# The ada_w partition sums: one float32 product per 512 columns, or two products on a high and a low part

## The chip, the cores and the metric

The kernel runs on one core of a Trainium2 chip. The metric is the device time of one execution in microseconds (us); the figure given is the median of several runs. A core has five engines that work side by side: TensorE (PE in the rows, with PEld for its weight loads), VectorE (DVE), ScalarE (ACT), GpSimd (POOL) and SyncE (SP, which issues most of the DMAs). Each engine takes its own instructions in the order in which the program lists them.

## The reference, cut to what matters

The program is two transformer blocks in a row over 256 tokens of width 2048: a mixer block with three branches and a feed-forward part, and a second block with four attention mixers and 16 experts. The change touches only how `mod` is made, with which the second block is modulated:

```
c_act = jax.nn.silu(c)
for l in range(DEPTH):
    mod = c_act @ ada_w[l] + ada_b[l]
    sh1, sc1, g1, sh2, sc2, g2 = jnp.split(mod, 6, axis=-1)
    h = rmsnorm_2(x, norm1_g[l]) * (1.0 + sc1[:, None]) + sh1[:, None]
    x = x + g1[:, None] * token_mixer(h, w_in[l], ...)
    ...
```

`c` has 2048 entries and `ada_w` is 2048 x 12288, so `mod` is six vectors of 2048. They depend on nothing of the first block, and the kernel computes them in the background while the first block runs.

## The kernel before, in words

Every large matrix product goes through one stream of chunks. A chunk is up to 1024 columns of one 128-row tile of a weight. SP loads the tile into a ring buffer; `_split` (L146, L147) then makes two parts of it, with the type float32r, which TensorE takes in one go: ACT casts it to a high part `wh`, and DVE subtracts that from the weight to get the low part `wl`. TensorE multiplies three times (`wh*xh`, `wh*xl`, `wl*xh`; L181 to L183, or L171 to L173 where tokens are on the partitions of the output). `run` keeps some four to five chunks split ahead of the one that TensorE works on, and after each chunk calls `step`, which takes one piece of background work from each queue: attention heads, norms, convolutions, and a queue named "ada". What `step` calls is recorded there and then, so its instructions stand in each engine's list behind the splits that are already ahead and in front of the splits still to come.

Tiles of `ada_w` are loaded in between as side loads, 96 of 1 MB each. They go through no split and no large product. For one of six groups `g`, 16 tiles are summed on DVE with the entries of `c` as factors (L1148) into `a`, a float32 tile of 128 x 2048 that holds the partial sums of each partition. When the 16th is in, `total(g)` is put on the queue "ada", two empty steps behind. `total` sums `a` over the partitions: for each of four pieces of 512 columns TensorE multiplies a column of ones with the piece (L1160; the result is one row of 512 in PSUM), and ACT copies the row back into partition 0 of `a` (L1161). GpSimd then writes the row to DRAM (L1163). This happens six times in the program, each time between two chunks of the large products.

The tags `pts` and `prob`, which the change borrows, are small tiles of 128 x 512 that the attention heads and convolutions use, four buffers each.

Of the kernel before, what the change touches and what calls it, by code (L numbers as in the profile page):

```python
# [10 lines left out]
F32 = mybir.dt.float32  # L11
F32R = mybir.dt.float32r
# [33 lines left out]
class Kernel:  # L46
# [1054 lines left out]
    def prepare2(self):  # L1101

        nc, i = self.nc, self.i
# [39 lines left out]
        def use(g, kt, wt):  # L1143
            if g == 0 and kt == 0:
                self.flush("norm", "c")
                start(0)
            a = A[g]
            nc.vector.scalar_tensor_tensor(a, wt, self.col["c"][:, kt:kt + 1], a, op0=OP.mult, op1=OP.add)  # L1148
            if kt == 15:
                if g < 5:  # L1150
                    start(g + 1)
                for f in 2 * [lambda: None] + [lambda: total(g)]:
                    self.bg("ada", f)

        def total(g):
            a = A.pop(g)
            for k in range(4):
                ps = self.bank()
                s = slice(k * 512, k * 512 + 512)
                nc.tensor.matmul(ps[0:1, :], self.ones[:, 0:1], a[:, s], start=True, stop=True)  # L1160
                nc.scalar.copy(a[0:1, s], ps[0:1, :])  # L1161
                self.done(ps)
            nc.gpsimd.dma_start(self.mod[order[g]:order[g] + 1, :], a[0:1, :])  # L1163
            self.free(a)
            if g == 1:
                self.later("ada", 2, lambda: self.setup_cols(first, 4))
            if g == 5:
                self.setup_cols(second)
# [1182 lines left out]
```

## Time and profile before

| what | value |
|---|---|
| median of 3 runs | 2854.59 us (2854.22 to 2856.4) |
| the profiled execution's own time | 2856.04 us |
| span of its instructions | 2854.3 us |
| PE busy | 2756.7 us, 97% of the span |
| DVE busy | 2106.4 us, 74% |
| ACT busy | 1418.5 us, 50% |
| POOL busy | 315.8 us, 11% |
| mean granted TensorE clock | 0.987 |

The profile is of one execution whose own time is 1.45 us above the median; 1.7 us of its time lie around the span. Busy shares are averages over stages with different limits. A matmul is recorded with a length that overlaps the next one, so the distance from the start of one to the start of the next tells what it costs in a stream. A float32 product is recorded as two matmuls, which is why L1160 has 48 records for 24 products.

### The profile page before, as it was taken

The page shows a single profiled execution, that of the slowest core. Times are in us where ns is not written, and L with a number is a line of the kernel's source. Part 1 is how long each engine was busy: PE and PEld are TensorE (multiplying, and loading weights), DVE is VectorE, ACT ScalarE, POOL GpSimd, SP SyncE. Part 2 cuts the span into 40 slices and gives each one's busy share as a digit, 9 for nine tenths or more (in the row PEclk, how much of TensorE's full clock was granted, in tenths as well). Part 3 has the DMA queues.
Part 4 walks back from the last instruction along what each step waited for, and adds up shares of the span by engine and source line. Part 5 has one row for each costly group of instructions (what it writes and reads, how often), then busy time and mean ns, then how long its engine had stood idle before and what let it go on. Part 6 is the DMA issues. An engine that isn't in the chain of part 4 may idle for free. (4 is left out here: it accounts for less than half of the span.)

```text
span 2854.3 us, 43859 instructions
## 1 busy us (share of the span) xinstructions
PE 2756.7 (97%) x17766; PEld 2410.4 (84%) x17766; DVE 2106.4 (74%) x2679; ACT 1418.5 (50%) x2100; POOL 315.8 (11%) x286
## 2 busy tenths in 40 slices
PE   8999999999999999999999998999999799999997
PEld 8898999999998999897989797988886676666664
DVE  5566558899767768877777786656555689998998
ACT  5433444334444545434444445345554476666665
POOL 0000100000100000001000102111001202222223
PEclk9999999999999999999999999999999899999999
DMA  7576555566667765676667573745555599989895
GB/s 256 193 275 247 199 215 166 176 235 214 248 233 266 259 228 221 239 263 216 257 216 267 195 253 128 265 128 195 179 202 173 209 372 337 342 324 343 322 342 211
DMA packets 201427, 685.77 MB, mean 240 GB/s; under 512 B 12148, under 2 KB 15332, under 8 KB 180356
## 3 DMA queue, kind: packets, MB, share of 16 engines
q1 hardware_dynamic: 194336, 662.94, 64.3%
q0 software_dynamic: 5680, 19.53, 2.5%
q8 instruction: 141, 2.31, 0.3%
q10 hardware_dynamic: 1203, 0.45, 0.1%
q14 instruction: 67, 0.54, 0.1%
HBM read 680.66 MB, written 2.20 MB: 239 GB/s over the span
## 5 line engine op out<-in xcount | busy, mean ns | idle before, releaser
L147 DVE TENSOR_TENSOR u<-u,u 128x1024 fp32r<-128x1024 f32 (+3 forms) x1064 | 1258.1, 1216 | 393.9 <-ACT u L146 392.2
L146 ACT CAST u<-u 128x1024 fp32r<-128x1024 f32 (+3 forms) x1064 | 1015.3, 995 | 615.6 <-DMA u<-in_w_in_dram 157.3
L181 PE MATMUL ps<-u,u 128*128 128x256 f32 (+1 forms) x2184 | 626.3, 287 | 2.6 <-ACT u L146 1.7
L183 PE MATMUL ps<-u,u 128*128 128x256 f32 (+1 forms) x2184 | 621.1, 284 | 2.5 <-DVE u L147 2.5
L182 PE MATMUL ps<-u,u 128*128 128x256 f32 (+1 forms) x2184 | 621.0, 284 | 0.5
L181 PE MATMUL ps<-big,u 128*128 128x256 f32 (+1 forms) x1672 | 481.4, 288 | 1.2 <-ACT big L1285 0.7
L183 PE MATMUL ps<-big,u 128*128 128x256 f32 (+1 forms) x1672 | 476.6, 285 | 4.3 <-DVE u L147 4.3
L182 PE MATMUL ps<-big,u 128*128 128x256 f32 (+1 forms) x1672 | 476.5, 285 | 0.1
L181 PEld LDWEIGHTS ps<-u,u 128*128 128x128 f32 (+1 forms) x2184 | 420.9, 193 | 11.9 <-issue 6.4
L183 PEld LDWEIGHTS ps<-u,u 128*128 128x128 f32 (+1 forms) x2184 | 420.7, 193 | 4.4 <-DVE u L147 4.3
L182 PEld LDWEIGHTS ps<-u,u 128*128 128x128 f32 (+1 forms) x2184 | 420.9, 193 | 1.7 <-DVE u L1286 1.3
L181 PEld LDWEIGHTS ps<-big,u 128*128 128x128 f32 (+1 forms) x1672 | 322.9, 193 | 13.5 <-issue 7.0
L183 PEld LDWEIGHTS ps<-big,u 128*128 128x128 f32 (+1 forms) x1672 | 322.9, 193 | 5.8 <-DVE u L147 5.6
L182 PEld LDWEIGHTS ps<-big,u 128*128 128x128 f32 (+1 forms) x1672 | 323.0, 193 | 1.1 <-DVE big L1286 0.6
L171 PE MATMUL ps<-u,u 128*128 128x512 f32 x736 | 291.6, 396 | 5.4 <-ACT u L146 5.3
L172 PE MATMUL ps<-u,u 128*128 128x512 f32 x736 | 288.8, 392 | 7.9 <-DVE u L147 7.5
L173 PE MATMUL ps<-u,u 128*128 128x512 f32 x736 | 287.6, 391 | 0.0
L1148 DVE SCALAR_TENSOR_TENSOR u<-u,cols,u 128x2048 f32<-128x2048 f32 x96 | 226.3, 2357 | 5.6 <-DMA u<-in_ada_w_dram 5.5
L1914 PE MATMUL ps<-u,xg 128*128 128x512 f32 x416 | 187.9, 452 | 0.4 <-DVE xg L1905 0.3
L172 PEld LDWEIGHTS ps<-u,u 128*128 128x128 f32 x736 | 138.7, 188 | 39.4 <-DVE u L147 12.4
L171 PEld LDWEIGHTS ps<-u,u 128*128 128x128 f32 x736 | 138.5, 188 | 39.5 <-ACT u L146 8.7
L1915 PE MATMUL ps<-u,xg 128*128 128x512 f32 x416 | 167.7, 403 | 0.8 <-DVE u L147 0.7
(374 smaller groups left out, 3111.5 us busy)
## 6 DMA issues: line engine op xcount, KB each, us to landing
u<-in_w_in_dram SPq DMA_DIRECT2D x128, 1024.0 KB, 5.0
u<-in_ada_w_dram SPq DMA_DIRECT2D x96, 1024.0 KB, 5.4
u<-in_w_up_dram SPq DMA_DIRECT2D x88, 1024.0 KB, 5.4
u<-in_exp_w_gate_dram SPq DMA_DIRECT2D x64, 1024.0 KB, 9.5
u<-in_exp_w_up_dram SPq DMA_DIRECT2D x64, 1024.0 KB, 6.8
u<-in_exp_w_down_dram SPq DMA_DIRECT2D x64, 1024.0 KB, 8.1
u<-in_w_down_dram SPq DMA_DIRECT2D x44, 1024.0 KB, 6.7
u<-in_w_o_dram SPq DMA_DIRECT2D x16, 1024.0 KB, 6.8
```

The costliest lines, as they stand in the source:

```text
L146: self.nc.scalar.copy(wh[:, :width], wt)
L147: self.nc.vector.tensor_sub(wl[:, :width], wt, wh[:, :width].bitcast(F32))
L171: nc.tensor.matmul(o, xh[:, ts], wh[:, cs], start=first, stop=False)
L172: nc.tensor.matmul(o, xh[:, ts], wl[:, cs], start=False, stop=False)
L173: nc.tensor.matmul(o, xl[:, ts], wh[:, cs], start=False, stop=last)
L181: nc.tensor.matmul(o, wh[:, cs], xh, start=first and m % 2 == 0, stop=False, **kw)
L182: nc.tensor.matmul(o, wh[:, cs], xl, start=False, stop=False, **kw)
L183: nc.tensor.matmul(o, wl[:, cs], xh, start=False, stop=last, **kw)
L1148: nc.vector.scalar_tensor_tensor(a, wt, self.col["c"][:, kt:kt + 1], a, op0=OP.mult, op1=OP.add)
L1914: self.nc.tensor.matmul(ps, x, wh[:, s], start=start, stop=False)
L1915: self.nc.tensor.matmul(ps, x, wl[:, s], start=False, stop=stop)
```

## The change

`total` makes a float32r column `one` out of the column of ones when it is first called. For each piece of 512 columns ACT then casts the piece to a high part `h` (in a `pts` buffer), DVE subtracts it from the piece to give a low part `l` (in a `prob` buffer), and TensorE multiplies the ones with `h` and with `l`, both summed in the same PSUM row. The copy back is as before.

```diff
         def total(g):
             a = A.pop(g)
+            if g == 0:
+                self.one = self.ctile([128, 1], "one", F32R)
+                nc.scalar.copy(self.one, self.ones[:, 0:1])
             for k in range(4):
                 ps = self.bank()
                 s = slice(k * 512, k * 512 + 512)
-                nc.tensor.matmul(ps[0:1, :], self.ones[:, 0:1], a[:, s], start=True, stop=True)
+
+                h, l = (self.small([128, 512], tag, 4, F32R) for tag in ("pts", "prob"))
+                nc.scalar.copy(h, a[:, s])
+                nc.vector.tensor_sub(l, a[:, s], h.bitcast(F32))
+                nc.tensor.matmul(ps[0:1, :], self.one, h, start=True, stop=False)
+                nc.tensor.matmul(ps[0:1, :], self.one, l, start=False, stop=True)
                 nc.scalar.copy(a[0:1, s], ps[0:1, :])
                 self.done(ps)
```

In the changed file the cast is L1165, the subtraction L1166, the two products L1167 and L1168, and the copy back L1169.

On ACT, at the first of the six sums (`u157` is the tile `a`, `u416` and `u422` are halves of chunks that are split ahead), the list before reads:

```order
L146 CAST u416_3538<-u392_3368 128x1024 [waits Activation_49]
L1161 COPY u157_1483<-ps418_3567 1x512 [waits DMASW3_49,PE_49]
L1161 COPY u157_1483<-ps419_3570 1x512 [waits PE_49]
L1161 COPY u157_1483<-ps420_3573 1x512 [waits PE_49]
L1161 COPY u157_1483<-ps421_3576 1x512 [waits PE_49]
L146 CAST u422_3580<-u404_3451 128x1024 [waits DMAHW7_49,Activation_49]
```

In the changed program the same place on ACT reads:

```order
L146 CAST u416_3538<-u392_3368 128x1024 [waits Activation_49]
L1159 CAST one_3567<-ones_77 128x1
L1165 CAST pts419_3570<-u157_1483 128x512 [waits DMASW3_49]
L1169 COPY u157_1483<-ps418_3569 1x512 [waits PE_49]
L1165 CAST pts422_3578<-u157_1483 128x512
L1169 COPY u157_1483<-ps421_3577 1x512 [waits PE_49]
L1165 CAST pts425_3586<-u157_1483 128x512
L1169 COPY u157_1483<-ps424_3585 1x512 [waits PE_49]
L1165 CAST pts428_3594<-u157_1483 128x512
L1169 COPY u157_1483<-ps427_3593 1x512 [waits PE_49]
L146 CAST u430_3602<-u404_3451 128x1024 [waits DMAHW7_49]
```

Each cast of a piece now stands behind the copy back of the piece ahead of it, and that copy waits for PE. The other five sums have the same pattern, without the cast of `one`.

On PE, at the same place, the four float32 products give way to eight, in pairs, between two chunks of the large product:

```order
-L1160 MATMUL ps418_3567<-u157_1483,ones_77 1x512 [waits DMASW3_49,DVE_49]
-L1160 MATMUL ps419_3570<-u157_1483,ones_77 1x512 [waits Activation_49]
-L1160 MATMUL ps420_3573<-u157_1483,ones_77 1x512 [waits DVE_49]
-L1160 MATMUL ps421_3576<-u157_1483,ones_77 1x512 [waits Activation_49]
+L1167 MATMUL ps418_3569<-pts419_3570,one_3567 1x512 [waits DVE_49,Activation_49]
+L1168 MATMUL ps418_3569<-prob420_3571,one_3567 1x512 [waits DVE_49]
+L1167 MATMUL ps421_3577<-pts422_3578,one_3567 1x512 [waits PE_49,Activation_49]
+L1168 MATMUL ps421_3577<-prob423_3579,one_3567 1x512 [waits DVE_49]
+L1167 MATMUL ps424_3585<-pts425_3586,one_3567 1x512 [waits Activation_49]
+L1168 MATMUL ps424_3585<-prob426_3587,one_3567 1x512 [waits DVE_49]
+L1167 MATMUL ps427_3593<-pts428_3594,one_3567 1x512 [waits Activation_49]
+L1168 MATMUL ps427_3593<-prob429_3595,one_3567 1x512 [waits DVE_49]
```

The second product of each pair waits for DVE's subtraction, and the next product of the large matrix stands behind the last of the eight.

On DVE, at the same place in the changed program, the four subtractions stand between two subtractions of the split:

```order
L147 TENSOR_TENSOR u416_3538<-u392_3368,u416_3538 128x1024 [waits Activation_49]
L1166 TENSOR_TENSOR prob420_3571<-u157_1483,pts419_3570 128x512 [waits Activation_49]
L1166 TENSOR_TENSOR prob423_3579<-u157_1483,pts422_3578 128x512 [waits Activation_49]
L1166 TENSOR_TENSOR prob426_3587<-u157_1483,pts425_3586 128x512 [waits Activation_49]
L1166 TENSOR_TENSOR prob429_3595<-u157_1483,pts428_3594 128x512 [waits PE_49,Activation_49]
L147 TENSOR_TENSOR u430_3602<-u404_3451,u430_3602 128x1024 [waits DMAHW7_49,Activation_49]
```

The first of them stands behind the split's subtraction ahead of it; before, nothing of the sums stood on DVE here.

## Rows read from the trace of the kernel before

**Rows 1.** The page's first part: busy time of PE.

```profile
PE 2756.7 (97%) x17766; PEld 2410.4 (84%) x17766; DVE 2106.4 (74%) x2679; ACT 1418.5 (50%) x2100; POOL 315.8 (11%) x286
```

**Rows 2.** Timeline of PE at the six sums: start, length, engine, line, [idle before].

```profile
361.05 3.59 PE L1160 MATMUL ps<-u,ones 128*1 128x512 f32 x8
364.57 0.39 PE L181 MATMUL ps<-u,u 128*128 128x256 f32 x1
...
784.16 3.59 PE L1160 MATMUL ps<-u,ones 128*1 128x512 f32 x8
...
1064.38 3.60 PE L1160 MATMUL ps<-u,ones 128*1 128x512 f32 x8
...
1349.33 3.59 PE L1160 MATMUL ps<-u,ones 128*1 128x512 f32 x8
...
1635.26 3.59 PE L1160 MATMUL ps<-u,ones 128*1 128x512 f32 x8
...
2014.71 3.59 PE L1160 MATMUL ps<-u,ones 128*1 128x512 f32 x8
```

**Rows 3.** Timeline of PE in a stream of float32r products of 512 columns.

```profile
1326.11 0.39 PE L172 MATMUL ps<-u,u 128*128 128x512 f32 x1
1326.33 0.39 PE L173 MATMUL ps<-u,u 128*128 128x512 f32 x1
```

**Rows 4.** Timeline of ACT, then of DVE, behind the fifth sum.

```profile
1638.88 0.58 ACT L1161 COPY u<-ps 1x512 f32<-1x512 f32 x1 [0.28 <-PE ps L1160]
1639.37 0.61 ACT L146 CAST u<-u 128x512 fp32r<-128x512 f32 x1
...
1640.01 0.69 DVE L147 TENSOR_TENSOR u<-u,u 128x512 fp32r<-128x512 f32 x1 [6.25 <-ACT u L146]
```

**Rows 5.** Timeline of DVE, then of PE, where PE waits for a subtraction.

```profile
1090.71 1.22 DVE L147 TENSOR_TENSOR u<-u,u 128x1024 fp32r<-128x1024 f32 x1
...
1091.98 0.38 PE L183 MATMUL ps<-u,u 128*128 128x256 f32 x1 [0.55 <-DVE u L147]
```

**Rows 6.** Timeline of ACT and DVE: their last work ahead of each sum.

```profile
359.96 1.03 ACT L146 CAST u<-u 128x1024 fp32r<-128x1024 f32 x1
...
361.03 1.23 DVE L147 TENSOR_TENSOR u<-u,u 128x1024 fp32r<-128x1024 f32 x1 [1.99 <-ACT u L146]
...
780.35 2.36 DVE L147 TENSOR_TENSOR u<-u,u 128x1024 fp32r<-128x1024 f32 x2 [4.62 <-ACT u L146]
...
1061.16 2.35 DVE L147 TENSOR_TENSOR u<-u,u 128x1024 fp32r<-128x1024 f32 x2
...
1350.37 2.35 DVE L147 TENSOR_TENSOR u<-u,u 128x1024 fp32r<-128x1024 f32 x2
...
1632.47 1.29 DVE L147 TENSOR_TENSOR u<-u,u 128x512 fp32r<-128x512 f32 x2
...
2011.92 1.28 DVE L147 TENSOR_TENSOR u<-u,u 128x512 fp32r<-128x512 f32 x2
```

**Rows 7.** Timeline of PE where it resumes behind waits for DVE.

```profile
692.28 0.77 PE L921 MATMUL ps<-ln,ones 128*128 128x256 f32 x1 [5.21 <-DVE ln L916]
...
1329.52 0.50 PE L172 MATMUL ps<-u,u 128*128 128x512 f32 x1 [0.99 <-DVE u L147]
```

**Rows 8.** Stretches: length, busy time of PE, PEld, DVE, ACT, POOL, PE's clock, DMA.

```profile
692.30:697.00 4.70, 4.70 (x20) 4.52 (x21) 4.31 (x3) 0.74 (x2) 0.00 (x0) 0.50 0.64 222
697.01:704.00 6.99, 6.99 (x60) 6.99 (x60) 4.47 (x3) 6.74 (x11) 0.00 (x0) 1.00 0.31 83
...
1188.97:1191.93 2.96, 2.96 (x7) 2.38 (x8) 2.96 (x3) 0.35 (x1) 0.00 (x0) 0.50 0.60 126
...
1329.50:1333.00 3.50, 3.48 (x15) 2.92 (x16) 3.50 (x3) 0.37 (x1) 0.00 (x0) 1.00 0.66 159
```

**Rows 9.** PE's waits in total: us, times, longest us.

```profile
PE ps L1836 <- DVE sel L1833: 9.5, 1, 9.5
...
PE ps L921 <- DVE ln L916: 5.2, 1, 5.2
```

## The prediction

> **What bounds the kernel now.** I began with the busy times: PE is busy 2756.7 of 2854.3 us, 97% [rows 1]. Whatever lengthens PE's list in a full stretch lengthens the kernel, and what ACT or DVE do costs only where PE comes to wait for it. Next I read PE's timeline at the six places of the change. The reader is to see that a sum stands in a full stream: at the first one the first product with the ones starts at 361.05 and the next chunk at 364.57, and no row there shows idle time; the other five look the same [rows 2]. So PE spends 3.52 us from the first product of a sum to the next chunk, six times, 21.1 us in all, and it waits for nothing there. Third, I read the timelines of ACT and DVE ahead of the sums, since the change puts them into PE's way. At four of six sums both have been idle for some time when PE arrives; at the first and the fourth DVE has just begun on splits [rows 6].
>
> **What the change removes.** Four float32 products per sum, 3.52 us of PE's time, six times [rows 2].
>
> **What it adds on PE.** Eight float32r products of 512 columns. In a stream these follow each other by 0.22 to 0.23 us [rows 3]. If nothing waited, a sum would take 8 x 0.23 = 1.84 us, 1.7 less than now.
>
> **What it adds as a wait.** The parts are not there beforehand. In ACT's list the cast of piece k+1 stands behind the copy back of piece k. That copy needs both products of piece k, and the second of them needs DVE's subtraction, which needs the cast. So four pieces go round one loop through three engines, and nothing of two pieces overlaps. The loop, from the start of one copy back to that of the next:
>
> - copy back to cast on ACT: 1638.88 to 1639.37, 0.49 us [rows 4];
> - cast of 128 x 512 and hand-off to DVE: 1639.37 to 1640.01, 0.64 us [rows 4];
> - subtraction of 128 x 512: 0.69 us [rows 4];
> - hand-off from DVE to PE: a subtraction from 1090.71 for 1.22 us, PE at 1091.98, so 0.05 us [rows 5];
> - the second product until its result can be read: 0.39 us [rows 3], and 0.04 for the hand-off, like the others.
>
> That is 2.30 us. The parts of the first piece can be made ahead of PE, and at sums 2, 3, 5 and 6 they are: DVE ends its last split at 782.71, 1063.51, 1633.76 and 2013.20, a subtraction of 0.69 later the low part is there, and PE arrives at 784.16, 1064.38, 1635.26 and 2014.71 [rows 2, 6]. There PE takes 0.23 for the first product, three loops of 2.30, 0.23 for the last product and about 0.1 to start on the next chunk: 7.4 us against 3.52, so 3.9 more.
>
> At sum 1 DVE works on a split from 361.03 for 1.23 us. A second one in a row starts 1.13 behind the first (two take 2.36, one 1.23) [rows 6], so the low part is there at 361.03 + 1.13 + 0.69 + 0.05 = 362.90, 1.85 us behind PE's arrival instead of 0.23: 1.6 on top, 5.5. ACT's cast ends at 360.99 and the cast of `one` and of the first piece fit beside DVE's split. At sum 4 DVE has two splits until 1352.72, so the low part is there at about 1353.37, 4.04 behind PE's arrival at 1349.33 [rows 2, 6]: 3.8 on top, 7.7.
>
> Sum of the loops: 4 x 3.9 + 5.5 + 7.7 = 28.8 us. Bounds: DVE's part could be a fifth longer where GpSimd works beside it, or the loop could be 0.2 shorter if hand-offs overlap. With 18 loops of 2.1 to 2.55 that is 25 to 33 us.
>
> **Edits at no cost.** The cast of `one` happens once. The buffers `pts` and `prob` have four slots each, and sums of four pieces take one round of them. The splits behind a sum are held up on ACT, but against PE they stay where they were: before, ACT's next split starts 0.6 us after PE resumes (1639.37 at the fifth sum [rows 4], where PE resumes at 1635.26 + 3.52 = 1638.78 [rows 2]); in the changed order it starts 0.49 behind the last copy back, which itself starts some 0.2 behind PE's restart, about 0.7. The chunks that PE takes meanwhile had been split ahead of the sum. If that cover were gone, PE would wait another 0.7 to 2 us per sum. The write to DRAM moves with the last copy back, and its readers come several steps later.
>
> **TensorE's clock.** During a loop PE does two products of 0.23 in 2.30 us, for some 7 us. What such a broken stretch does to the clock, the trace shows at neighbours. Behind a wait of 5.21 us PE resumed at 692.28 and ran at half clock (0.50, that is 1.2 instead of 2.4 GHz) until 697: 20 products in 4.70 us, which at full clock (60 in 6.99) take 2.3, so 2.4 us lost. Elsewhere, among waits of about 1 us for a split, PE ran at 0.50 from 1188.97 to 1191.93: 7 products of 512 in 2.96 us instead of 1.6, 1.4 lost. Yet behind a wait of 0.99 us at 1329.52 the clock stayed at 1.00 [rows 3, 7, 8]. A sum of the changed kernel is idle longer than the first of these in total, and is broken for longer than any of them, so I take the fall as likely at each of the six, at the mean of both prices, 1.9 us: 11.4 us. Bounds: 0 (as at 1329.52) and 6 x 2.4 = 14.4.
>
> The Trainium skill, "TensorE: Matmul & The Clock Gate", section "HAM oscillation — how this bites in real kernels", says that a matmul loop with idle gaps between its bursts is put back to the half clock and that each next burst then starts slow. [...]
>
> **Sum.** 28.8 + 11.4 = 40.2 us. On the profiled execution's own 2856.04 that is 2896.2; its time is 1.45 above the median, and on the median of 2854.59 it is 2894.8. I predict 2895.
>
> **Rivals.**
>
> - *The loop without the clock.* The small products keep the clock at 1.00. For it: 1329.52. Against: 692.30 and 1188.97 [rows 8]. Time: 2854.6 + 28.8 = 2883.
> - *The products get cheaper and nothing waits.* Two float32r passes for a float32 product: 1.84 against 3.52 us, 1.7 less, six times: 10 us less, 2844.5. It decides if the parts of a piece are there before PE wants them, that is if ACT casts ahead of its copies back. Against: the order on ACT, with a copy back between any two casts.
> - *The delay is taken up later.* PE has waits of 5.2 and 9.5 us for DVE behind the sums [rows 9]. If DVE came to these by its own pace, they would shrink as PE gets late: up to 14.7 us back, 2880. Against: DVE's work there uses what PE has just made, and it moves along.
> - *The splits come too late as well.* ACT and DVE take up the splits behind a sum later than PE needs them; at 1091.98 PE already waits for a split soon after the third sum [rows 5]. Four subtractions more on DVE, 2.8 us, would come on top at two or three sums: 2895 + 7 = 2902.
>
> **How the numbers follow.** Loop with clock 0.68 (2886 to 2902 by its own bounds), loop without clock 0.15, late splits 0.08, taken up later 0.04, cheaper products 0.03, no measurable change by a mixture 0.02. The range of 2881 to 2904 leaves out the last two, the strongest form of the third last and the tail of the late splits. A measurement of this kernel tells about 0.2% (5.7 us) from no change. Slower holds all but the last two: 0.95; faster 0.03; same 0.02.
>
> **What would show it.** Right: at each sum PE's timeline shows the second product of a pair waiting for DVE, pairs 2.3 us apart, and 7.4 us from the first product to the next chunk (9 and 11 at the first and fourth sum); ACT alternates cast and copy; the clock reads 0.50 behind the sums. PE's total wait for L1166 would be near 6 x 6 = 36 us. Wrong: pairs 0.5 us apart, a clock of 1.00 throughout, or shrunken waits at L921 and L1836.

## The result and the profile after

The changed kernel takes 2897.25 us (median of 4 runs, 2895.84 to 2898.7); before, beside it, 2854.56 us (4 runs). That is 42.7 us more, a ratio of 1.0147 with an interval of 1.0131 to 1.0163. The kernel before, run again beside the experiments, had medians of 2856.31 and 2856.09, so a difference between the change and an experiment is uncertain by some 2 us. The profiled execution took 2898.02 us with a span of 2896.2 us.

The page's first part answers to [rows 1]. PE is busy 12 us longer in a span that is 42 us longer; most of the loss is PE standing still.

```profile
PE 2768.5 (96%) x17766; PEld 2421.3 (84%) x17766; DVE 2123.0 (73%) x2703; ACT 1432.0 (49%) x2125; POOL 316.2 (11%) x286
```

PE's timeline at the second sum answers to the second place of [rows 2]. Columns are start, length, engine, line, tiles, shape, and in brackets the idle time ahead with its releaser.

```profile
791.85 0.28 PE L183 MATMUL ps<-u,u 128*128 128x256 f32 x1
791.97 0.40 PE L1167 MATMUL ps<-pts,one 128*1 128x512 f32 x1
792.20 0.40 PE L1168 MATMUL ps<-prob,one 128*1 128x512 f32 x1
793.79 0.40 PE L1167 MATMUL ps<-pts,one 128*1 128x512 f32 x1 [1.18 <-ACT pts L1165]
794.51 0.39 PE L1168 MATMUL ps<-prob,one 128*1 128x512 f32 x1 [0.33 <-DVE prob L1166]
796.09 0.39 PE L1167 MATMUL ps<-pts,one 128*1 128x512 f32 x1 [1.18 <-ACT pts L1165]
796.82 0.40 PE L1168 MATMUL ps<-prob,one 128*1 128x512 f32 x1 [0.34 <-DVE prob L1166]
798.39 0.58 PE L1167 MATMUL ps<-pts,one 128*1 128x512 f32 x1 [1.18 <-ACT pts L1165]
799.12 0.58 PE L1168 MATMUL ps<-prob,one 128*1 128x512 f32 x1
799.50 0.41 PE L181 MATMUL ps<-u,u 128*128 128x256 f32 x1
```

The second products of the four pairs start at 792.20, 794.51, 796.82 and 799.12, that is 2.30 to 2.31 apart. From the first product (791.97) to the next chunk (799.50) are 7.53 us, against 3.52 in [rows 2]. The first pair waits for nothing. The last two products are longer (0.58), and so are the chunk's (0.41): the clock has fallen while PE was still in the loop.

ACT at the same place, and below "..." DVE, show what goes round:

```profile
792.64 0.57 ACT L1169 COPY u<-ps 1x512 f32<-1x512 f32 x1 [2.95 <-PE ps L1168]
793.12 0.61 ACT L1165 CAST pts<-u 128x512 fp32r<-128x512 f32 x1
794.94 0.57 ACT L1169 COPY u<-ps 1x512 f32<-1x512 f32 x1 [1.21 <-PE ps L1168]
...
793.77 0.69 DVE L1166 TENSOR_TENSOR prob<-u,pts 128x512 fp32r<-128x512 f32 x1 [2.55 <-ACT pts L1165]
```

Copy at 792.64, cast 0.48 later, subtraction 0.65 after that, product at 794.51 (0.74), next copy at 794.94 (0.43): 2.30 in all. ACT sits idle for 1.21 us of each lap, with the next cast ready to go behind a copy that waits for PE.

At the fourth sum PE comes to a cast that is not there. PE's timeline, and below "..." that of ACT:

```profile
1368.08 0.28 PE L183 MATMUL ps<-big,u 128*128 128x256 f32 x1
1371.13 0.59 PE L1167 MATMUL ps<-pts,one 128*1 128x512 f32 x1 [2.77 <-ACT pts L1165]
1372.66 0.59 PE L1168 MATMUL ps<-prob,one 128*1 128x512 f32 x1 [0.94 <-DVE prob L1166]
1374.43 0.59 PE L1167 MATMUL ps<-pts,one 128*1 128x512 f32 x1 [1.18 <-ACT pts L1165]
1375.16 0.59 PE L1168 MATMUL ps<-prob,one 128*1 128x512 f32 x1
...
1380.53 0.41 PE L181 MATMUL ps<-big,u 128*128 128x256 f32 x1
...
1368.56 1.99 ACT L146 CAST u<-u 128x1024 fp32r<-128x1024 f32 x2 [6.61 <-DVE u L1071]
1370.46 0.61 ACT L1165 CAST pts<-u 128x512 fp32r<-128x512 f32 x1
```

Two split casts, 1.99 us together, stand ahead of the cast of the piece. They stood there before as well, over PE's arrival at 1349.33 [rows 2]; the timeline of ACT in the kernel before:

```profile
1348.16 1.99 ACT L146 CAST u<-u 128x1024 fp32r<-128x1024 f32 x2 [4.43 <-DVE u L1148]
```

The clock falls during PE's wait (0.59 from 1371.13 on), and the laps are longer by it: 1372.66 to 1375.16 is 2.50.

For a table of all six sums I take the time from the start of the last chunk product ahead of a sum to that of the first one behind it. Before it is 3.73 us at each (783.95 to 787.68 at the second). After, in the profiled execution:

| sum | 1 | 2 | 3 | 4 | 5 | 6 | all |
|---|---|---|---|---|---|---|---|
| after, us | 9.74 | 7.65 | 7.66 | 12.45 | 7.84 | 7.84 | |
| more than before | 6.0 | 3.9 | 3.9 | 8.7 | 4.1 | 4.1 | 30.8 |
| predicted | 5.5 | 3.9 | 3.9 | 7.7 | 3.9 | 3.9 | 28.8 |

Of the 18 laps seven ran at half clock and took 2.50 (two at sum 1, three at sum 4, the last one each at sums 5 and 6). At 0.2 us each that is 1.4 of the 2.0 us that the loops cost more than predicted.

The clock is read from windows: stretch, length, busy time of PE, PEld, DVE, ACT, POOL, then the granted clock, DMA share, GB/s. The first row is ahead of the second sum, the next six are behind sums 2, 1, 3, 4, 5 and 6, and the last is elsewhere:

```profile
787.00:791.80 4.80, 4.80 (x42) 4.80 (x42) 2.96 (x3) 2.69 (x4) 0.00 (x0) 1.00 0.55 197
...
799.50:804.20 4.70, 4.70 (x24) 4.69 (x23) 2.90 (x3) 4.36 (x5) 0.49 (x1) 0.50 0.02 5
...
371.00:374.00 3.00, 3.00 (x16) 3.00 (x15) 1.23 (x1) 1.41 (x2) 0.49 (x1) 0.50 0.01 3
...
1085.42:1087.00 1.58, 1.58 (x9) 1.58 (x8) 0.00 (x0) 1.33 (x2) 0.48 (x1) 0.50 0.00 0
...
1380.60:1384.50 3.90, 3.90 (x20) 3.90 (x19) 2.17 (x2) 3.73 (x5) 0.49 (x1) 0.50 0.01 2
1672.40:1674.50 2.10, 2.10 (x12) 2.10 (x11) 0.83 (x2) 1.95 (x4) 0.49 (x1) 0.50 0.00 1
...
2057.60:2059.50 1.90, 1.90 (x11) 1.90 (x10) 0.34 (x1) 1.05 (x2) 0.51 (x1) 0.50 0.00 0
...
1348.20:1350.60 2.40, 2.40 (x7) 1.90 (x6) 2.40 (x3) 0.00 (x0) 0.00 (x0) 0.53 0.71 177
```

The clock is 0.50 (1.2 GHz) behind every sum. What that costs I read by the lag: the start of one product of the large matrix after, less its start before. Behind sum 2 the first chunk product lags by 11.82 (787.68 and 799.50) and one further on by 13.78 (790.42 and 804.20): 2.0 lost. Read where the clock is back at 1.00, the loss behind the six sums is 1.48, 2.03, 0.87, 1.69, 0.96 and 1.26, together 8.3 us. The last row is a place that ran at 1.00 before [rows 8]; there 1.3 are lost (1329.52 and 1347.58, 1331.23 and 1350.62). Such places win and lose, net 2.8 us. The lag at the end is 41.9 = 30.8 + 8.3 + 2.8.

PE's waits in total (us, times, longest) answer to [rows 9]:

```profile
PE ps L1167 <- ACT pts L1165: 24.6, 20, 2.8
...
PE ps L1844 <- DVE sel L1841: 9.5, 1, 9.5
...
PE ps L921 <- DVE ln L916: 5.2, 1, 5.2
...
PE ps L1168 <- DVE prob L1166: 3.8, 8, 0.9
```

The long waits are as before to a tenth. The new ones are 28.4 us together.

### The profile page after: what moved, and what is told of

Same layout as the page of the kernel before. It is cut to its first block, busy times and chain, and to the rows that moved or that the text cites. A ratio compares the mean times of both kernels' runs of the same rounds, so it can differ in the third digit from the quotient of the medians.

```text
span 2896.2 us, 43896 instructions
## 1 busy us (share of the span) xinstructions
PE 2768.5 (96%) x17766; PEld 2421.3 (84%) x17766; DVE 2123.0 (73%) x2703; ACT 1432.0 (49%) x2125; POOL 316.2 (11%) x286
## 3 DMA queue, kind: packets, MB, share of 16 engines
q8 instruction: 141, 2.31, 0.3%
## 5 line engine op out<-in xcount | busy, mean ns | idle before, releaser
L181 PEld LDWEIGHTS ps<-big,u 128*128 128x128 f32 (+1 forms) x1672 | 324.3, 194 | 11.4 <-issue 7.3
L1148 DVE SCALAR_TENSOR_TENSOR u<-u,cols,u 128x2048 f32<-128x2048 f32 x96 | 226.3, 2357 | 5.0 <-DMA u<-in_ada_w_dram 4.9
```

The costliest lines, as they stand in the source:

```text
L181: nc.tensor.matmul(o, wh[:, cs], xh, start=first and m % 2 == 0, stop=False, **kw)
```

## Experiments

The theory: the time is lost in a loop of ACT, DVE and PE, closed by the order on ACT (the cast of a piece behind the copy back of the one ahead), and in the half clock that the broken stretch brings. The rivals: the extra casts and subtractions cost by themselves, since the splits come late; the clock costs nothing.

### The parts made, but not used (`parts_unused`)

The casts and subtractions stay; the products are the old ones, on the float32 tile, so the parts go nowhere.

```diff
-                nc.tensor.matmul(ps[0:1, :], self.one, h, start=True, stop=False)
-                nc.tensor.matmul(ps[0:1, :], self.one, l, start=False, stop=True)
+                nc.tensor.matmul(ps[0:1, :], self.ones[:, 0:1], a[:, s], start=True, stop=True)
```

> The casts and subtractions of the change are made in the same places, but the product is the float32 one on the unsplit piece; the parts are not used. Theory (the loop through ACT, DVE and PE costs the time, not the work in it): PE has nothing new to wait for, so 3.5 us per sum as before and 2854 to 2857 us in all. Rival (the 24 casts and 24 subtractions themselves cost: ACT and DVE fall behind with the splits, 24 x 1.3 us of engine time): 2865 to 2885 us, with PE waiting for splits behind the sums.

Measured: 2862.16 us (11 runs, 2857.96 to 2864.85) against 2856.31, ratio 1.0017 [1.0008, 1.0026]. This is 5 us above what the theory gave and 3 below the rival's least. All six sums take 3.73 as before. ACT and DVE still take turns: at the third sum ACT's copies back start 1.91 us apart (1065.13, 1067.04, 1068.95), each but the first behind a wait for the subtraction. PE is not in that loop and is through at 1067.60. Most of the loss is at one place behind this sum, where PE waits for a split; PE's timeline, and below "..." a window:

```profile
1092.52 0.38 PE L181 MATMUL ps<-u,u 128*128 128x256 f32 x1 [1.61 <-ACT u L146]
...
1094.79 0.58 PE L183 MATMUL ps<-u,u 128*128 128x256 f32 x1 [1.77 <-DVE u L147]
...
1095.00:1100.00 5.00, 5.00 (x24) 5.00 (x25) 2.85 (x4) 2.89 (x4) 1.29 (x1) 0.50 0.61 206
```

In [rows 5] the same place has one wait of 0.55. The lag rises by 5.3 us here (-0.3 to 5.0); 1 us is won back soon after, and another 2.8 come behind 2110, far from the sums, where stretches at half clock lie. So the work of the parts, the borrowed buffers included, costs a few us where PE is on time, and the rest of the 42.7 comes from PE waiting for them. In the changed kernel even this is missing: PE comes late there itself, and the lag shrinks from 18.39 to 17.68.

### Casts ahead of the copies back (`cast_ahead`)

The parts of piece k+1 are listed ahead of the products and the copy back of piece k. The work is the same; the loop is cut open.

```diff
+            hl = split(0)
             for k in range(4):
...
+                h, l = hl
+                if k < 3:
+                    hl = split(k + 1)
                 nc.tensor.matmul(ps[0:1, :], self.one, h, start=True, stop=False)
```

> As the change, but the cast and subtraction of piece k+1 are listed ahead of the products and the copy back of piece k. Theory (the place of the cast behind the copy back makes the loop): two pieces are then under way at once, one piece per 1.15 us instead of 2.30; a sum takes about 3.9 us at four places, 5.5 and 7.7 at the first and fourth, and the clock stays at 1.00 at most of them: 2858 to 2868 us. Rival (the float32r products of one column, or the half clock that they bring, cost the time wherever the casts stand): within 10 us of the change, 2887 to 2897.

Measured: 2864.84 us (11 runs, 2859.59 to 2867.69), ratio 1.0026 [1.0017, 1.0035], 32.4 us below the change. PE's timeline at the second sum, and below "..." at the fourth:

```profile
786.27 0.40 PE L1175 MATMUL ps<-pts,one 128*1 128x512 f32 x1
...
788.09 0.39 PE L1175 MATMUL ps<-pts,one 128*1 128x512 f32 x1 [0.72 <-ACT pts L1164]
788.81 0.39 PE L1176 MATMUL ps<-prob,one 128*1 128x512 f32 x1 [0.34 <-DVE prob L1165]
...
790.04 0.28 PE L181 MATMUL ps<-u,u 128*128 128x256 f32 x1
...
1352.59 0.40 PE L1175 MATMUL ps<-pts,one 128*1 128x512 f32 x1 [1.34 <-ACT pts L1164]
1355.26 0.59 PE L1176 MATMUL ps<-prob,one 128*1 128x512 f32 x1 [2.27 <-DVE prob L1165]
```

At sums 2, 3, 5 and 6 a sum now takes 3.9 and the clock stays up (the chunk's products are 0.28). Sum 1 takes 5.74 and sum 4 8.16: there the first parts come late. These two, 6.4 us, are most of the lag of 8.2 at the end. The order on ACT is thus most of the loss. But the cheaper products bring nothing yet: the cast of the third piece still stands behind the copy back of the first, and PE waits for it (0.72).

### The loop's gaps filled (`filled`)

Eight products whose result is overwritten stand ahead of the products of pieces 2 to 4. The loop stays; PE is busy in it.

```diff
             for k in range(4):
+                if k:
+                    p = h
...
+                for _ in range(8 if k else 0):
+                    nc.tensor.matmul(ps[0:1, :], self.one, p, start=True, stop=True)
```

> As the change, but in the wait of each of pieces 2 to 4 PE does eight extra products of the ones with the high part of the piece before (overwritten, the sums are as before), 1.8 us of work in a wait of about 1.9. Theory (the clock falls because PE is idle in the loop, and that is a quarter of the cost): the clock stays at 1.00 at the six sums, the loops stay at 2.3 us, and 8 to 11 us are gained: 2885 to 2890 us. Rival (the half clock at the sums costs nothing, since PE waits anyway): 2895 to 2899 us. Another (one column of ones does not keep the clock up): 0.50 at the sums as before and 2897 to 2905 us.

Measured: 2883.31 us (4 runs, 2881.19 to 2884.24), ratio 1.0092 [1.0076, 1.0107], 13.9 us below the change with 144 more products. PE's timeline in the second sum, and below "..." windows in that sum and behind the fourth:

```profile
789.75 2.01 PE L1170 MATMUL ps<-pts,one 128*1 128x512 f32 x8
791.60 0.40 PE L1171 MATMUL ps<-pts,one 128*1 128x512 f32 x1
791.84 0.40 PE L1172 MATMUL ps<-prob,one 128*1 128x512 f32 x1
...
789.28:796.71 7.43, 7.43 (x34) 2.58 (x32) 2.08 (x3) 3.29 (x6) 0.00 (x0) 1.00 0.33 128
...
1372.60:1380.00 7.40, 7.40 (x64) 7.40 (x63) 5.71 (x5) 4.37 (x5) 0.50 (x1) 1.00 0.31 102
```

The laps are 2.32 (789.51 to 791.84 to 794.16), the clock is 1.00 in and behind the sums, and a sum that isn't late takes 7.55. The six take 26.5 more than before, and the lag at the end is 27.1. So the clock is worth some 14.8 us of lag: 4.3 in the sums, 8.3 behind them, some 2 elsewhere. Of the 4.3, 3.0 are at sum 4 (9.43 against 12.45), where in this kernel the cast was there in time (1362.16, the product at 1363.23); that part need not be the clock's. Without it 12 us are left.

### The copy back on DVE (`copy_on_dve`)

```diff
-                nc.scalar.copy(a[0:1, s], ps[0:1, :])
+                nc.vector.tensor_copy(a[0:1, s], ps[0:1, :])
```

> As the change, but DVE copies the result row back instead of ACT. ACT then lists the four casts one behind the other with nothing of PE between them, and the loop is on DVE: a subtraction stands behind the copy back of the piece before. Theory (the loop is made by what stands between two pieces on one queue): the cast's 0.64 us leave the loop, a lap is subtraction 0.69 + hand-off 0.05 + product 0.43 to 0.63 + copy back about 0.6, so 1.7 to 2.0 us instead of 2.3 to 2.5; three laps at six sums give 7 to 12 us back, and the clock still falls: 2884 to 2891 us. Rival (the loop needs ACT's part, or is not what costs): 2895 to 2900 us.

Measured: 2886.73 us (4 runs, 2882.75 to 2887.33) against 2856.09, ratio 1.0097 [1.008, 1.0115]. ACT now has four casts in a row, and the loop moves to DVE, where the subtraction of a piece stands behind the copy back of the one ahead. DVE's timeline at the second sum:

```profile
790.28 0.68 DVE L1169 COPY u<-ps 1x512 f32<-1x512 f32 x1 [1.43 <-PE ps L1168]
790.89 0.67 DVE L1166 TENSOR_TENSOR prob<-u,pts 128x512 fp32r<-128x512 f32 x1
792.04 0.68 DVE L1169 COPY u<-ps 1x512 f32<-1x512 f32 x1 [0.48 <-PE ps L1168]
```

Laps are 1.76 (790.28 to 792.04), 0.55 shorter, since the cast is out of them. The six sums take 20.3 more than before, 10.5 less than in the change, and the medians differ by the same 10.5. The clock falls at all six all the same. A shorter loop is a loop still.

### The parts a step ahead (`two_steps`)

The sum becomes two halves. The parts of two pieces are made one background step ahead of their products, in a tile of their own; the next group's tile is therefore started only when a sum is done.

```diff
-                if g < 5:
-                    start(g + 1)
-                for f in 2 * [lambda: None] + [lambda: total(g)]:
-                    self.bg("ada", f)
+                for n in range(2):
+                    for f in (parts, total):
+                        self.bg("ada", lambda f=f, n=n: f(g, n))
...
+            self.free(A.pop(g), H.pop(g))
+            if g < 5:
+                start(g + 1)
```

> The parts of two pieces are made one background step ahead of their products, for pieces 1 and 2 and then for 3 and 4, so PE should find them ready; the tile of the next group is started behind the last product instead of ahead of the first. Theory (with the parts ready, two float32r products cost less than one float32 product): 4 x 0.23 + 0.1 us twice per sum, 2.1 against 3.5 us, 8 us less than before in all: 2844 to 2850 us, faster than both kernels. Rival (something else of the change costs, the products or the buffers): 2855 us or more, with PE waiting at the sums.

Measured: 2852.45 us (11 runs, 2849.82 to 2858.93), ratio 0.9988 [0.9978, 0.9997]. That is short of the gain expected. PE's timeline at the fourth sum shows why:

```profile
1343.20 0.40 PE L1175 MATMUL ps<-u,one 128*1 128x512 f32 x1 [2.00 <-ACT u L1166]
1345.41 0.59 PE L1176 MATMUL ps<-u,one 128*1 128x512 f32 x1 [1.81 <-DVE u L1167]
```

The two waits are 3.8 us together (the expectation of the next run says 5.8). One step is too little there: ACT takes up the casts at 1342.53, when the last DVE addition of the group (L1148) is through, and PE is there before. The same happens, smaller, at the first sum (1.27 and 0.33 us, where that expectation says 3.0).

### The parts two steps ahead (`parts_two_ahead`)

```diff
-                for n in range(2):
-                    for f in (parts, total):
-                        self.bg("ada", lambda f=f, n=n: f(g, n))
+                wait = lambda: None
+                for f in (lambda: parts(g, 0), wait, lambda: (total(g, 0), parts(g, 1)), lambda: total(g, 1)):
+                    self.bg("ada", f)
```

> As the version with the parts one step ahead, but the parts of pieces 1 and 2 are made two steps ahead of their products, in place of one. Theory (its 2852 us come from two places, the first and the fourth sum, where PE waited 3.0 and 5.8 us for the first parts and the clock fell once; the other four gave 1.85 us each): both waits lose 2.9 us, and 2845 to 2849 us come out, faster than the kernel before by 0.2 to 0.35%. Rival (the extra casts and subtractions on ACT and DVE hold up the splits, wherever they stand): no better than 2852.

Measured: 2850.89 us (10 runs, 2848.67 to 2853.87) against 2856.09, ratio 0.998 [0.9971, 0.9989]. This is faster than both kernels: 0.2% below before, 46 us below the change. It misses the range expected by 2 us, and by the total alone it is only 1 us better than the rival's bound. PE's timeline in the first half of the second sum:

```profile
782.76 0.40 PE L1175 MATMUL ps<-u,one 128*1 128x512 f32 x1
782.99 0.39 PE L1176 MATMUL ps<-u,one 128*1 128x512 f32 x1
783.22 0.40 PE L1175 MATMUL ps<-u,one 128*1 128x512 f32 x1
783.45 0.40 PE L1176 MATMUL ps<-u,one 128*1 128x512 f32 x1
783.69 0.28 PE L181 MATMUL ps<-u,u 128*128 128x256 f32 x1
```

The pairs are 0.46 apart and PE loses at most 0.3 us at any one wait for a part. The first half takes 0.93 us and the second (786.57 to 787.50) as much: 1.86 against 3.52 for the float32 products. By the lag the six sums gain 1.3 to 1.9 each, 10 us, against the rival. Only 4.9 are left at the end (5.2 by the medians): PE, early, meets other waits and stretches at half clock (2.6 us behind 1324, 3 between 1928 and 1967, 1.5 behind 2140), against 3 won between 1836 and 1877. It was not tried to have the parts still further ahead; that would keep the next group's tile waiting longer.

## Why the prediction held, step by step

- **The loop** was predicted with a lap of 2.30 us and measured at 2.30 to 2.31. A sum whose parts are begun in time was put at 7.4 us and took 7.53 (7.72 at sums 5 and 6, with a lap at half clock). `cast_ahead`, with the same work in another order, takes the loop away, and with it most of the half clock behind the sums and 32.4 of the 42.7 us; `copy_on_dve` shortens the lap and takes just that. That the order on the in-order engines makes the loss is shown by both.
- **Sums 1 and 4** were put at 1.6 and 3.8 on top and cost 2.1 and 4.8. At sum 1 the mechanism was as told (DVE stands in a split): the second product starts at 362.98, where 362.90 was forecast, and the rest is two laps of 2.50. At sum 4 I looked at DVE's splits and not at ACT's: PE waited 2.77 us for the cast itself and 0.94 for the subtraction. That made the second product 4.37 us late (1372.66 less 1349.33 and the lag of 18.96), where 4.04 was forecast; half clock in the loop, in three laps of 2.50, made most of the rest.
- **The clock** was put at 11.4 us, six falls at 1.9. It fell six times. Right behind the sums this cost 8.3 us, 0.9 to 2.0 each: part of each half-clock stretch lay inside the loop, where PE was waiting anyway. What made up for it was not in the sum: 2.8 us net at places far from the sums, and longer laps. The errors cancel in part: the loops came 2.0 us above their term, the clock behind the sums 3.1 below its own, and 2.8 came from places in no term. That the total is so near (41.9 by the lag, 40.2 forecast) is in part luck. `filled` shows 12 to 15 us for the clock in all. The Trainium skill, "TensorE: Matmul & The Clock Gate", section "HAM oscillation — how this bites in real kernels", tells of a matmul loop put back to the half clock by waits that are longer than any here. The waits in these loops were 1.18 us at most at five sums and 2.77 at the fourth, so it is the rows (0.50 behind each sum) that show the falls, and not that section.
- **The cheaper products.** 1.84 us in a stream was right (1.86 in `parts_two_ahead`), and so was the condition for it. With casts merely listed one piece ahead it was not yet met, since the casts of the last two pieces still stood behind copies back.
- **Late splits** exist (`parts_unused`), behind one sum, some 5.3 us, but in the change PE is itself so late that they cost nothing. **The delay taken up later** is out: the waits of 5.2 and 9.5 us are the same to a tenth.
- **A sign that I had told wrongly:** PE's wait for the subtraction, L1166, was to be near 36 us. It is 3.8, and 24.6 for the cast. In a loop the first product of a pair waits for the cast, and then what is left for the second is 0.3 us. And the 36 us counted the products' own time as waiting.

## What to carry to other kernels

When a piece of work is cut into steps on three engines, write down the list of each in-order engine: a result's copy back ahead of the next piece's first step closes a loop, and its lap, not the cost of the products, is the price. Moving a step to another engine can move the loop along with it. The gain of cheaper products is there only if their inputs are made far enough ahead that PE never waits, and a small gain on PE may be half taken back by waits and clock stretches elsewhere.

## What the runs showed that I had not expected

- Products with a single column of ones as the weight kept the clock up in a dense row: in `filled` 32 of them lie between 789.28 and 796.71, at 1.00. So 144 products with no use made the kernel 13.9 us faster than the change.
- Half clock makes not only products longer but the loop as well: 2.50 against 2.30 us per lap, since the product stands in it (0.59 against 0.40).
- Half-clock stretches far from the change come and go when PE's work is moved by some us: 1348.20 to 1350.60 has 0.53, the same chunks had 1.00 before [rows 8]. A gain or loss of 2 to 4 us of this kernel may be only that.
